# A decoder block in Strassen-like blocks: forming the sums of blocks behind the transpose instead of ahead of it

## The chip, the cores and the metric

The kernel runs on one core of a Trainium2 chip. The metric is the device time of one execution in microseconds, as the median of several runs. The core's engines work side by side, each through its own queue in order, and wait for each other by semaphores: TensorE (PE in the profile; its weight loads are PEld), VectorE (DVE), ScalarE (ACT) and GpSimd (POOL). SyncE (SP) only issues DMAs. SBUF is the on-chip memory, PSUM the eight banks into which TensorE writes; a bank holds 128 x 512 fp32.

## The reference

A block over 1024 tokens of width 1024, all in fp32: half a gated feed-forward layer, a mixer of attention and pooling, and another half feed-forward layer.

```python
h = x
h = h + 0.5 * swiglu(rms_norm(h, ffn1_norm), ffn1_w1, ffn1_w3, ffn1_w2)
u = rms_norm(h, mix_norm)
proj = u @ w_in                      # q, k, v, pooling input, two gates
...
h = h + merged @ w_out
h = h + 0.5 * swiglu(rms_norm(h, ffn2_norm), ffn2_w1, ffn2_w3, ffn2_w2)
return rms_norm(h, final_norm)
```

The three products that matter here are those with a normed `h` on one side: `ffn1_w1`/`ffn1_w3`, `w_in`, and `ffn2_w1`/`ffn2_w3`.

## The kernel before

**Seven products instead of eight.** Each large product is cut into two by two blocks and done with seven block products. The normed activations `X` are cut into `b11`, `b12`, `b21`, `b22`: tokens 0 to 511 or 512 to 1023, columns 0 to 511 (`LOWS`) or 512 to 1023 (`HIGHS`). The first index is the half of the columns, the second the half of the tokens. Needed are `b11`, `b21`, `b22` and four sums: `t1 = b12 - b11`, `t2 = b22 - t1`, `t4 = t2 - b21`, `t3 = b22 - b12`. A product of index `m` uses 1: `b11`, 2: `b21`, 3: `b22`, 4: `t4`, 5: `t1`, 6: `t2`, 7: `t3`, and the products run in the order 1, 6, 2, 7, 5, 4, 3.

**Three matmuls for one.** An operand is rounded to a high part (`hi`, type fp32r, by ScalarE's `AF.Copy`) and a low part (`lo`, the rest, by a subtraction on VectorE or GpSimd). Each product is hi x hi, hi x lo and lo x hi: 12 matmuls of 128 x 128 by 512 for a block of weights (`Sevens.product`, L314). `Sevens.split` (L303 high, L306 low) does this for the weights; inside an entry its low part is always GpSimd's.

**Rows and columns.** The normed rows come with tokens on the partitions, and TensorE needs columns there. So `Rows` transposes 128 x 512 by four TensorE operations against a unit matrix into one PSUM bank (L381), ScalarE writes the high part from the bank (L382), and `lower` writes the low part, bank minus high part, on VectorE (L385).

**An entry.** Each of the three layers begins with an entry. Tokens 0 to 511 (tiles 0 to 3) are normed and transposed first, giving `b11` and `b21`; their rows stay in `h[0]` to `h[3]`. Then `Entry.run` goes over the tiles t = 4 to 7 of the other tokens. While TensorE does products 1 and 2 of the first few weight blocks (`self.todo`: 12 products in the first feed-forward layer, of which 4 are done earlier, 8 in the others), it makes the sums of tile t with those of tile t - 4. The order is written out by hand (`manual_schedule`), and each engine's queue follows it. For one tile it is:

- a product `i`; the statistics of the next tile (`high(t + 1, 0)`, L263 and L264); transposes of `b22` and its high part;
- `t1`, `t2`, `t4` on VectorE (L423 to L425) and `t3` on GpSimd (L426), all on rows in SBUF; `b22`'s low part (L385);
- the weights of product `i + 2` (`operand`, L303, L306), the output of product `i`, the product `k = i + 1`, the weights of product `k + 2`;
- transposes of `t1`, `t2`, `t4`, `t3` with their high parts (L381, L382); scaling of the next tile's rows (`high(t + 1, 1)`, L267, on VectorE); the four low parts (L385); the output of `k`; squares for a later tile.

At t = 6 and 7 the first operands of the products behind the entry are prepared as well (`more`; their sums are L345, L347 and L351).

PSUM has two tags of four banks: `mm` (products 1, 2, 3, 5) and `acc` (the other products, and the transposes). The rows of tiles 0 to 3 are transposed in the last steps of the stage ahead: `rows` in `begin_up1` for the first entry, `rows_first` as tasks of the steps of the first down projection (its matmuls are L706), `rows_first2` and `lower` between the steps of the output projection (L1854).

Of the kernel before, what the change touches and what calls it, by code (L numbers as in the profile page):

```python
# [126 lines left out]
def tile_block(  # L127
# [40 lines left out]
    def bank(tag, name):  # L168
        return psum.tile([P, HALF], F32, tag=tag, name=name)
# [12 lines left out]
    ident = consts.tile([P, P], F32, name="ident")  # L182
# [5 lines left out]
    h = []  # L188
# [80 lines left out]
    def scaled_part(t, c, gain):  # L269
        ve.scalar_tensor_tensor(h[t][:, c], h[t][:, c], inv[t][:, 1:2], gain[:, c], op0=OP.mult, op1=OP.mult)  # L270
# [12 lines left out]
    LOWS, HIGHS = slice(0, HALF), slice(HALF, S)  # L283

    def sums_of_x(pool, name, order, **kw):
        return {
            s: tuple(pool.tile([P, 4, HALF], F32R, name=f"x{part}_{s}_{name}", **kw) for part in ("hi", "lo"))
            for s in order
        }

    class Sevens:


        def __init__(self, name, X, fw, fs=None):
            self.name, self.X, self.fw, self.fs = name, X, fw, fs or fw
            self.n_lo = 0
# [22 lines left out]
    class Quad:  # L319
# [51 lines left out]

    class Rows:


        def __init__(self, X, what, src, t, tag="acc"):
            q = t % 4
            self.hi, self.lo = (v[:, :, q * P:(q + 1) * P] for v in X[what])
            p = bank(tag, f"x_{what}_{t}")
            self.p = p.rearrange("p (k q) -> p k q", k=4)
            for k in range(4):  # L380
                pe.transpose(self.p[:, k, :], src[:, k * P:(k + 1) * P], ident)  # L381
            ac.activation(self.hi, self.p, AF.Copy)  # L382

        def lower(self):
            ve.tensor_tensor(self.lo, self.p, self.hi.bitcast(F32), op=OP.subtract)  # L385

    class Entry:

# [17 lines left out]
        def run(self, high, after, first=0):  # L406


            X = self.sv.X
            y = high(4, 1)  # L410
            for t in range(4, NT):
                i = first + 2 * (t - 4)
                k = i + 1
                self.product(i)
                if t + 1 < NT:
                    high(t + 1, 0)
                lo = self.low[t - 4]
                b11, b21, b12, b22 = lo[:, LOWS], lo[:, HIGHS], y[:, LOWS], y[:, HIGHS]
                s = Rows(X, "b22", b22, t)

                t1, t3 = b11, b21
                t2, t4 = (self.sv.half_tile("s", f"{n}_{t}") for n in ("t2", "t4"))
                ve.tensor_tensor(t1, b12, b11, op=OP.subtract)  # L423
                ve.tensor_tensor(t2, b22, t1, op=OP.subtract)
                ve.tensor_tensor(t4, t2, b21, op=OP.subtract)  # L425
                gp.tensor_tensor(t3, b22, b12, op=OP.subtract)  # L426
                s.lower()
                self.operand(i + 2)
                self.out(i)
                self.product(k)  # L430
                self.operand(k + 2)
                rs = [Rows(X, what, src, t) for what, src in (("t1", t1), ("t2", t2), ("t4", t4), ("t3", t3))]
                if t + 1 < NT:
                    y = high(t + 1, 1)
                for r in rs:
                    r.lower()
                self.out(k)
                after(t)
                if t >= NT - 2:
                    self.more(t - NT + 2)  # L440
# [318 lines left out]
    X = sums_of_x(scope.enter_context(sbuf("x1")), "f1", SUMS)  # L759
# [32 lines left out]
    def begin_up1():  # L792


        load_all()
        idle = bank("mm", "idle")

        def keep_on(n):

            for _ in range(n):  # L800
                pe.matmul(idle[:, :P], ones, ones, start=True, stop=True)

        def widen(b):
            k = slice(4 * b, 4 * b + 4)
            ve.tensor_copy(columns[:, k], gain1[:, k, None].to_broadcast([P, 4, P]))

        def gains(b):

            p = bank("acc", f"gain{b}")
            for k in range(4):  # L810
                pe.transpose(p[:, k * P:(k + 1) * P], columns[:, 4 * b + k], ident)
            return p

        r = {}

        def rows(t, what, c):
            scaled_part(t, c, gain_row)
            r[t] = Rows(X, what, h[t][:, c], t)

        keep_on(12)  # L820
        widen(0)
        squares(0, square)
        widen(1)
        inverse(0)
        g = [gains(b) for b in range(2)]
        keep_on(2)
        ve.tensor_copy(gain_row[:, LOWS], g[0])
        squares(1, square)
        squares(2, square)
        rows(0, "b11", LOWS)  # L830
        inverse(1)
        keep_on(2)
        inverse(2)
        squares(3, square)
        rows(1, "b11", LOWS)
        r[0].lower()
        keep_on(3)
        rows(2, "b11", LOWS)
        inverse(3)
        r[1].lower()  # L840
        keep_on(3)
        pairs = [Pair(sv1, j, sums, True, j == 2) for j in range(3)]
        entry = pre_run(sv1, [(q, m) for m in (1, 2) for q in pairs[:2]] + [(pairs[2], m) for m in (1, 2)],
                        pairs[0], h[:4])
        entry.operand(0)
        rows(3, "b11", LOWS)
        r[2].lower()
        keep_on(2)
        r[3].lower()
        ve.tensor_copy(gain_row[:, HIGHS], g[1])  # L850
        entry.product(0)
        entry.operand(1)

        square2 = columns_tile
        squares(4, square2)
        for t in (0, 1):
            rows(t, "b21", HIGHS)
        entry.product(1)
        entry.out(0)
        entry.operand(2)  # L860
        entry.operand(3)
        inverse(4)
        r[0].lower()
        for t in (2, 3):
            rows(t, "b21", HIGHS)
            r[t - 1].lower()
        entry.product(2)
        entry.out(1)
        squares(5, square2)
        r[3].lower()  # L870
        entry.product(3)
        entry.operand(4)
        entry.out(2)
        entry.operand(5)
        entry.out(3)

        def high(t, part):
            if part == 0:
# [12 lines left out]
        entry.run(high, after, 4)  # L891
        return pairs
# [308 lines left out]
    with sbuf("steps1", "right") as pool:  # L1201
# [30 lines left out]
        def rows_first(t, tag):  # L1232
            rs = [Rows(X_mix, "b11", h[t][:, LOWS], t, tag), Rows(X_mix, "b21", h[t][:, HIGHS], t, tag)]
            for r in rs:
                r.lower()

        def after1(m, t):
            if m == len(DOWN) - 3:
# [53 lines left out]
    with tc.manual_schedule():  # L1292
# [4 lines left out]
        for k in range(len(items) + 4):  # L1297
# [5 lines left out]
            if k < len(items):  # L1303
                q, m = items[k]
# [3 lines left out]
            if k - 1 in results:  # L1308
                q, m = items[k - 1]
# [404 lines left out]
    with tc.manual_schedule():  # L1714
# [44 lines left out]
        q = N // 2  # L1759
# [33 lines left out]
    op = wo.enter_context(sbuf("ops", "right"))  # L1793
# [83 lines left out]
    def scaled2(t):  # L1877
        scaled(t, h[t] if t < 4 else rows_y[t], gain2)

    def lower(rs):  # L1880
        for r in rs:
            r.lower()

    with tc.manual_schedule():
        for k in range(6):
# [59 lines left out]
        raws.load()  # L1945
        r = [rows_first2(t) for t in range(2)]
        step_o(STEPS - 3, range(2))
        lower(r[0])
        lower(r[1])
        r.append(rows_first2(2))  # L1950
        step_o(STEPS - 3, range(2, 4))
        lower(r[2])
        r.append(rows_first2(3))
        adds_o(m - 1, range(2))
        lower(r[3])
        adds_o(m - 1, range(2, 4))
        entry2.operand(0)
        entry2.operand(1)
# [172 lines left out]
```

## Time and profile before

| what | value |
|---|---|
| runs of the kernel | 1960.0, 1959.36, 1956.06 us; median 1959.36 |
| profiled execution, first to last instruction | 1955.6 us, mean granted TensorE clock 0.994 |
| its own time as listed | not marked among the runs; the nearest is 1956.06 |
| TensorE, weight loads | 1914.1, 1579.7 us busy |
| VectorE, ScalarE, GpSimd | 1343.5, 759.4, 741.1 us busy |
| DMA | 333.57 MB, mean 171 GB/s |

The profile comes from one execution. "Busy" counts an instruction from its start to its end, and on VectorE and GpSimd this includes time in which it stands still inside. The time line gives for each group of instructions its start, its length, engine, line, output and inputs, and in brackets how long the engine had been idle and which instruction released it. `x4` means four in a row merged. A table of windows gives, for each stretch of time, its length and the busy time of each engine with the number of instructions, then the granted clock of TensorE and the DMA's share and rate. The first entry's `Entry.run` starts its products at 28.16 us, the mixer's at 666.37 and the second feed-forward layer's at 1297.04.

### The profile page before, as it was taken

What the parts mean: (1) busy time and instruction counts of PE and PEld (TensorE: products, weight loads), DVE (VectorE), ACT (ScalarE), POOL (GpSimd) and SP (SyncE); (2) the same over time, 40 slices, a digit from 0 to 9 for tenths busy, and PEclk for the clock granted to TensorE, in tenths of its full rate; (3) what the DMA queues carried; (4) which work ended last, traced back from release to release, by engine and by line L of the source; (5) the groups of instructions that cost most, each with busy time, mean ns of one, the idle gap of its engine ahead of it and who ended that gap; (6) DMA issues with size and microseconds to landing.
All of it is one profiled execution on the core that took longest, in us unless ns stands there. A gap on an engine that the chain in (4) does not pass through costs nothing. (4 is left out here: it accounts for less than half of the span.)

```text
span 1955.6 us, 25018 instructions
## 1 busy us (share of the span) xinstructions
PE 1914.1 (98%) x8938; PEld 1579.7 (81%) x8938; DVE 1343.5 (69%) x2012; ACT 759.4 (39%) x1361; POOL 741.1 (38%) x557
## 2 busy tenths in 40 slices
PE   9999999999999999999998999999999999999997
PEld 7788888888888887888876878887788888878885
DVE  7776556557686876568774886887665556577766
ACT  6333333334344533334344662253333333333343
POOL 5333333332222444445454365543333333322231
PEclk9999999999999999999998999999999999999999
DMA  4155223336465546765658887643523223454653
GB/s 185 44 194 169 85 86 117 121 124 208 156 246 201 167 120 230 232 220 185 232 218 289 241 241 261 253 161 96 190 102 135 82 87 120 139 204 135 212 195 142
DMA packets 147005, 333.57 MB, mean 171 GB/s; under 512 B 20160, under 2 KB 40896, under 8 KB 145344
## 3 DMA queue, kind: packets, MB, share of 16 engines
q1 hardware_dynamic: 138096, 308.00, 45.9%
q10 hardware_dynamic: 8784, 23.96, 3.5%
q8 instruction: 71, 1.16, 0.2%
q14 instruction: 54, 0.44, 0.1%
HBM read 229.61 MB, written 102.30 MB: 170 GB/s over the span
## 5 line engine op out<-in xcount | busy, mean ns | idle before, releaser
L706 PE MATMUL d_f<-bhi_f,alo_f 128*128 128x512 f32 x616 | 240.8, 391 | 2.4 <-POOL alo_f L668 2.2
L706 PE MATMUL d_f<-bhi_f,ahi_f 128*128 128x512 f32 x616 | 240.9, 391 | 0.2 <-ACT ahi_f L664 0.2
L706 PE MATMUL d_f<-blo_f,ahi_f 128*128 128x512 f32 x616 | 240.0, 390 | 0.0
L668 POOL TENSOR_TENSOR alo_f<-g_f,ahi_f 128x512 fp32r<-128x512 f32 x70 | 99.2, 1434 | 298.5 <-ACT ahi_f L664 289.8
L314 PE MATMUL u_mixm<-xhi_t_mix,wc_mixm 128*128 128x512 f32 x608 | 196.0, 393 | 2.7 <-POOL wc_mixm L306 2.3
L314 PE MATMUL u_mixm<-xhi_b_mix,wc_mixm 128*128 128x512 f32 x456 | 149.3, 393 | 2.0 <-DVE y_m L982 2.0
L706 PEld LDWEIGHTS d_f<-bhi_f,alo_f 128*128 128x128 f32 x616 | 115.7, 188 | 29.0 <-POOL alo_f L668 4.0
L314 PEld LDWEIGHTS u_mixm<-xhi_t_mix,wc_mixm 128*128 128x128 f32 x608 | 113.8, 188 | 29.0 <-POOL wc_mixm L306 4.9
L706 PEld LDWEIGHTS d_f<-bhi_f,ahi_f 128*128 128x128 f32 x616 | 115.8, 188 | 24.1 <-ACT ahi_f L664 0.6
L706 PEld LDWEIGHTS d_f<-blo_f,ahi_f 128*128 128x128 f32 x616 | 115.8, 188 | 23.8
L314 PE MATMUL u_mixm<-xlo_t_mix,wc_mixm 128*128 128x512 f32 x304 | 118.6, 390 | 0.0
L306 POOL TENSOR_TENSOR wc_mixm<-s_mixm,wc_mixm 128x512 fp32r<-128x512 f32 x52 | 75.8, 1459 | 99.7 <-ACT wc_mixm L303 84.0
L314 PEld LDWEIGHTS u_mixm<-xhi_b_mix,wc_mixm 128*128 128x128 f32 x456 | 85.7, 188 | 20.7 <-ACT late_hi L1125 2.8
L303 ACT ACTIVATE wc_mixm<-s_mixm 128x512 fp32r<-128x512 f32 x76 | 47.6, 629 | 122.8 <-DVE s_mixm L347 52.1
L314 PE MATMUL u_mixm<-xlo_b_mix,wc_mixm 128*128 128x512 f32 x228 | 88.9, 390 | 0.0
L664 ACT ACTIVATE ahi_f<-g_f 128x1024 fp32r<-128x1024 f32 x84 | 81.8, 974 | 2.0 <-DMA g_f<-gs_f 2.0
L306 POOL TENSOR_TENSOR wc_mixm<-raw,wc_mixm 128x512 fp32r<-128x512 f32 x40 | 60.4, 1515 | 44.9 <-ACT wc_mixm L303 42.0
L664 ACT ACTIVATE bhi_f<-s_f2w 128x512 fp32r<-128x512 f32 x55 | 32.8, 627 | 97.1 <-DVE s_f2w L684 86.8
L1854 PE MATMUL wo<-w_o,o_hi 128*128 128x512 f32 x224 | 69.3, 391 | 0.0
L314 PEld LDWEIGHTS u_mixm<-xlo_t_mix,wc_mixm 128*128 128x128 f32 x304 | 57.2, 188 | 11.7 <-DVE xlo_t_mix L385 0.2
L664 ACT ACTIVATE bhi_f<-s_f1w 128x512 fp32r<-128x512 f32 x55 | 32.9, 630 | 85.1 <-DVE s_f1w L684 80.2
L1616 PE MATMUL yp<-pool_in,wab 128*128 128x512 f32 x192 | 55.7, 426 | 4.2 <-DMA pool_in<-pool 4.2
(1300 smaller groups left out, 5099.8 us busy)
## 6 DMA issues: line engine op xcount, KB each, us to landing
g_f<-gs_f SPq DMA_DIRECT2D x70, 512.0 KB, 4.5
gs_f<-y_f SPq DMA_DIRECT2D x88, 256.0 KB, 2.3
raw<-in_w2a_dram SPq DMA_DIRECT2D x35, 512.0 KB, 4.1
raw<-in_w2b_dram SPq DMA_DIRECT2D x35, 512.0 KB, 4.0
gs_f<-gb_f SPq DMA_DIRECT2D x46, 256.0 KB, 2.3
raw<-in_w1a_dram SPq DMA_DIRECT2D x22, 512.0 KB, 4.6
raw<-in_w3a_dram SPq DMA_DIRECT2D x22, 512.0 KB, 6.3
raw<-in_w1b_dram SPq DMA_DIRECT2D x22, 512.0 KB, 4.5
```

The costliest lines, as they stand in the source:

```text
L303: ac.activation(w[:, 0], src, AF.Copy)
L306: eng.tensor_tensor(w[:, 1], src, w[:, 0].bitcast(F32), op=OP.subtract)
L314: pe.matmul(p, a, b, start=(start and k == 0 and q == 0), stop=(k == 3 and q == 2), skip_group_check=not start)
L664: ac.activation(hi[:, c], src, AF.Copy)
L668: eng.tensor_tensor(lo[:, d], src[:, o], hi[:, d].bitcast(F32), op=OP.subtract)
L706: pe.matmul(self.banks[m][t], l, r, start=(first and q == 0), stop=(last and q == 2))
L1616: pe.matmul(p, a, b, start=(j == 0), stop=(j == 11))
L1854: pe.matmul(banks[m][t], l, r, start=(st == 0 and j == 0 and q == 0), stop=(st == 1 and j == 1 and q == 2))
```

## The change

In `Entry.run` only `b12` and `b22` of a tile are transposed (both ahead of product `k`), and the sums are formed from the transposed blocks: `t1` from the bank of `b12`, `t2` from the bank of `b22`, `t4` and `t3` in SBUF from `t2`. `t1` and `t2` are then half tiles in SBUF, `t3` and `t4` take the places of `b11` and `b21`. A new class `Parts` takes a high part (ScalarE) and a low part (VectorE, for `t3` GpSimd) from such an fp32 block in SBUF. For that `b11` and `b21` of tiles 0 to 3 must be there transposed: `Rows.keep` copies their bank into `h[t]` on ScalarE, 8 times in each entry. `b22`'s low part moves behind product `k`; one transpose of the first entry takes its bank from `mm`. The formula for `t3` becomes `t2 - b11`, which is the same sum. In the changed program `t1` to `t4` are L441, L442, L445 and L444, `Parts` is L398 (high) and L401 (low), `keep` is L389.

```diff
@@ class Rows
-            p = bank(tag, f"x_{what}_{t}")
+            p = self.flat = bank(tag, f"x_{what}_{t}")
...
+        def keep(self, dst):
+            ac.activation(dst.rearrange("p (k q) -> p k q", k=4), self.p, AF.Copy)
+
+    class Parts:
+        def __init__(self, X, what, src, t, eng):
+            q, self.eng = t % 4, eng
+            self.hi, self.lo = (v[:, :, q * P:(q + 1) * P] for v in X[what])
+            self.src = src.rearrange("p (k q) -> p k q", k=4)
+            ac.activation(self.hi, self.src, AF.Copy)
+
+        def lower(self):
+            self.eng.tensor_tensor(self.lo, self.src, self.hi.bitcast(F32), op=OP.subtract)

@@ Entry.run
-                lo = self.low[t - 4]
-                b11, b21, b12, b22 = lo[:, LOWS], lo[:, HIGHS], y[:, LOWS], y[:, HIGHS]
-                s = Rows(X, "b22", b22, t)
-
-                t1, t3 = b11, b21
-                t2, t4 = (self.sv.half_tile("s", f"{n}_{t}") for n in ("t2", "t4"))
-                ve.tensor_tensor(t1, b12, b11, op=OP.subtract)
-                ve.tensor_tensor(t2, b22, t1, op=OP.subtract)
-                ve.tensor_tensor(t4, t2, b21, op=OP.subtract)
-                gp.tensor_tensor(t3, b22, b12, op=OP.subtract)
-                s.lower()
+                b11, b21 = (self.low[t - 4][:, c] for c in (LOWS, HIGHS))
+                p12 = bank("acc", f"x_b12_{t}")
+                for j in range(4):
+                    c = slice(j * P, (j + 1) * P)
+                    pe.transpose(p12[:, c], y[:, c], ident)
+                s = Rows(X, "b22", y[:, HIGHS], t)
+
+                t1, t2 = (self.sv.half_tile("s", f"{n}_{t}") for n in ("t1", "t2"))
+                ve.tensor_tensor(t1, p12, b11, op=OP.subtract)
+                ve.tensor_tensor(t2, s.flat, t1, op=OP.subtract)
+                rs = [Parts(X, "t2", t2, t, ve)]
+                gp.tensor_tensor(b11, t2, b11, op=OP.subtract)
+                ve.tensor_tensor(b21, t2, b21, op=OP.subtract)
+                rs[0].lower()
                 self.operand(i + 2)
                 self.out(i)
                 self.product(k)
                 self.operand(k + 2)
-                rs = [Rows(X, what, src, t) for what, src in (("t1", t1), ("t2", t2), ("t4", t4), ("t3", t3))]
                 if t + 1 < NT:
                     y = high(t + 1, 1)
+                s.lower()
+                rs = [Parts(X, what, src, t, eng) for what, src, eng in (("t1", t1, ve), ("t4", b21, ve), ("t3", b11, gp))]
                 for r in rs:
                     r.lower()

@@ begin_up1
-        rows(3, "b11", LOWS)
+        rows(3, "b11", LOWS, "mm")
...
         entry.product(0)
         entry.operand(1)
+        for t in range(4):
+            r[t].keep(h[t][:, LOWS])
...
         squares(5, square2)
         r[3].lower()
+        for t in range(4):
+            r[t].keep(h[t][:, HIGHS])
         entry.product(3)
         entry.operand(4)

@@ rows_first, and lower(t, rs) of the output projection alike
             for r in rs:
                 r.lower()
+            for r, c in zip(rs, (LOWS, HIGHS)):
+                r.keep(h[t][:, c])
```

More of the change, by code (lines that the diff above doesn't have):

```diff
@@ L814, in begin_up1, with rows @@
         r = {}
-        def rows(t, what, c):
+        def rows(t, what, c, tag="acc"):
             scaled_part(t, c, gain_row)
-            r[t] = Rows(X, what, h[t][:, c], t)
+            r[t] = Rows(X, what, h[t][:, c], t, tag)
         keep_on(12)
@@ L1878, in scaled2, with lower @@
         scaled(t, h[t] if t < 4 else rows_y[t], gain2)
-    def lower(rs):
+    def lower(t, rs):
         for r in rs:
             r.lower()
+        for r, c in zip(rs, (LOWS, HIGHS)):
+            r.keep(h[t][:, c])
     with tc.manual_schedule():
@@ L1947, in tile_block @@
         step_o(STEPS - 3, range(2))
-        lower(r[0])
-        lower(r[1])
+        lower(0, r[0])
+        lower(1, r[1])
         r.append(rows_first2(2))
         step_o(STEPS - 3, range(2, 4))
-        lower(r[2])
+        lower(2, r[2])
         r.append(rows_first2(3))
         adds_o(m - 1, range(2))
-        lower(r[3])
+        lower(3, r[3])
         adds_o(m - 1, range(2, 4))
```

## The prediction

> **What bounds the kernel now.** I read the page first, then the windows of the three entries, then the order in time inside one of them.
>
> ```profile
> span 1955.6 us, 25018 instructions
> PE 1914.1 (98%) x8938; PEld 1579.7 (81%) x8938; DVE 1343.5 (69%) x2012; ACT 759.4 (39%) x1361; POOL 741.1 (38%) x557
> ...
> core 0: us, PE busy (x) PEld busy (x) DVE busy (x) ACT busy (x) POOL busy (x), PEclk, DMA share, GB/s
> 28.16:59.78 31.62, 31.25 (x178) 26.18 (x176) 27.77 (x37) 18.89 (x36) 20.91 (x15) 1.00 0.15 51
> 666.37:697.59 31.22, 30.87 (x178) 26.33 (x176) 27.20 (x38) 18.91 (x37) 19.58 (x14) 1.00 0.14 51
> 1297.04:1328.86 31.82, 31.18 (x177) 26.25 (x176) 28.18 (x40) 19.08 (x35) 17.41 (x12) 1.00 0.20 70
> ```
>
> Over the whole span TensorE is the bound at 98%. The change touches little besides the three windows, each from an entry's first product to the first product behind it: 94.7 us of the 1955.6. In them VectorE is busy 27 to 28 of 31 to 32 us and GpSimd 17 to 21: two engines close behind the first. Now one token tile of the first entry, in order of time.
>
> ```profile
> 28.16 0.39 PE L314 MATMUL u_f10a<-xhi_b_f,wc_f10a 128*128 128x512 f32 x1
> ...
> 30.88 0.60 PE L381 MATMUL x_b<-ident,x 128*128 128x128 f32 x4
> 31.23 0.48 PE L314 MATMUL u_f10b<-xhi_b_f,wc_f10b 128*128 128x512 f32 x1
> ...
> 38.96 0.48 PE L314 MATMUL u_f11b<-xhi_b_f,wc_f11b 128*128 128x512 f32 x1
> ...
> 40.63 1.30 POOL L426 TENSOR_TENSOR x<-x 128x512 f32<-128x512 f32 x1 [1.13 <-DVE s_f1t L425]
> 41.07 1.94 DVE L267 SCALAR_TENSOR_TENSOR x<-x,nst,gain_ffn 128x1024 f32<-128x1024 f32 x1
> 41.82 0.60 PE L381 MATMUL x_t<-ident,x 128*128 128x128 f32 x4
> 41.89 2.27 POOL L306 TENSOR_TENSOR wc_f12a<-raw,wc_f12a 128x512 fp32r<-128x512 f32 x1
> 43.08 2.48 DVE L385 TENSOR_TENSOR xlo_t_f<-x_t,xhi_t_f 128x512 fp32r<-128x512 f32 x4
> 43.48 0.47 PE L314 MATMUL u_f12a<-xhi_b_f,wc_f12a 128*128 128x512 f32 x1
> 44.12 1.29 POOL L306 TENSOR_TENSOR wc_f12b<-raw,wc_f12b 128x512 fp32r<-128x512 f32 x1
> 44.21 0.30 PEld L314 LDWEIGHTS u_f12a<-xhi_b_f,wc_f12a 128*128 128x128 f32 x2 [0.46 <-POOL wc_f12a L306]
> 46.99 0.48 PE L314 MATMUL u_f12b<-xhi_b_f,wc_f12b 128*128 128x512 f32 x1
> ...
> 54.70 0.48 PE L314 MATMUL u_f12b<-xhi_b_f,wc_f12b 128*128 128x512 f32 x1
> ```
>
> Columns are start, length, engine, line. A product of 12 matmuls takes 2.72 (28.16 to 30.88), four transposes 0.35 (to 31.23), sixteen 1.66 (41.82 to 43.48): a tile needs 2 x 2.72 + 0.35 + 1.66 = 7.45 of TensorE, and the intervals between second products (31.23, 38.96, 46.99, 54.70) are 7.73, 8.03 and 7.71. The 0.46 at 44.21 is TensorE's weight load waiting for the low part of a weight from GpSimd (L306). So GpSimd's queue is already the next bound, by a hair.
>
> Why is one L306 2.27 long and its neighbour 1.29? These rows tell:
>
> ```profile
> 14.65 1.28 POOL L306 TENSOR_TENSOR wc_f10b<-raw,wc_f10b 128x512 fp32r<-128x512 f32 x1 [0.24 <-ACT wc_f10b L303]
> 24.11 1.27 DVE L267 SCALAR_TENSOR_TENSOR x<-x,nst,gain_ffn 128x1024 f32<-128x1024 f32 x1
> 27.22 1.74 POOL L306 TENSOR_TENSOR wc_f10b<-raw,wc_f10b 128x512 fp32r<-128x512 f32 x1
> 27.84 1.67 DVE L425 TENSOR_TENSOR s_f1t<-s_f1t,x 128x512 f32<-128x512 f32 x1
> 39.13 0.69 DVE L424 TENSOR_TENSOR s_f1t<-x,x 128x512 f32<-128x512 f32 x1
> 63.38 1.28 POOL L306 TENSOR_TENSOR wc_f10a<-s_f10a,wc_f10a 128x512 fp32r<-128x512 f32 x1 [4.07 <-ACT wc_f10a L303]
> 63.86 1.35 DVE L306 TENSOR_TENSOR wc_f10a<-s_f10a,wc_f10a 128x512 fp32r<-128x512 f32 x1 [1.28 <-ACT wc_f10a L303]
> ```
>
> Alone, GpSimd's operation takes 1.28, L267 1.27, VectorE's half tile 0.69. Where a VectorE operation with two SBUF inputs meets one of GpSimd, the later is lengthened until the earlier is done: L306 on VectorE (63.86) ends 0.55 after GpSimd's at 64.66, about its own working time, L425 0.55 after 28.96. The four L385 at 43.08, with one input in PSUM, run beside GpSimd (44.12, 1.29) and neither is lengthened. So they take turns whenever both of VectorE's inputs are in SBUF, and not when one is in PSUM. The Trainium skill, "SBUF — State Buffer", section "SBUF: two separate sides", states this as a lock held for the whole instruction by a VectorE operation with two SBUF inputs or by GpSimd; it speaks against this change, whose new low parts have both inputs in SBUF. By that rule each meeting costs what the sum below takes; the trace agrees (1.35 for 0.69).
>
> **The change, part by part.**
>
> *Transposes.* Per tile 20 become 8 (the program's order: four into `x_b12`, four into `x_b22`, none later). Twelve at 1.66/16 are 1.25; over 12 tiles TensorE's work falls by 15.0 us. That is the whole gain, and it counts only where TensorE is the bound.
>
> *The turns.* Spacing of back-to-back operations: VectorE half tile (2.48 - 0.69)/3 = 0.60; GpSimd 1.25, an estimate from its 1.28 less the overlap with the next; L267 1.2. Before, a tile's turn-taking work is t1, t2, t4 (1.8), L267 (1.2), and on GpSimd t3, two L306 (3.75) and a small power (0.5): 7.3, just below TensorE's 7.45. After, t1 and t2 read PSUM and leave the turns, but t4 stays and the low parts of t2, t1, t4 join: 4 x 0.60 + 1.2 = 3.6 on VectorE. GpSimd has t3, two L306 and the low part of t3: 5.0. Together 8.6. VectorE's t1 (0.6), t2 (0.7, behind t1), the product's output and the statistic (0.7) do not need turns, but they stand in VectorE's queue exactly when GpSimd has little ready: t3 waits for t2, and the weights' high parts stand behind the high part of t2 on ScalarE. So a tile takes from 8.6 (full overlap) to 10.6 (none). I take 10.6 for the first entry and 10.0 for the others, whose outputs are mostly ScalarE's: the walk through the queues finds t1 of the next tile waiting for the low part of t4 of this one. TensorE, needing 6.2, waits twice per tile: for the weight's high part, then its low part.
>
> *First interval* (tiles 4 to 5): no backlog. From the second product: t1, t2, t4 1.9, t3 1.25, low part of t2 0.6, L306 1.3 = 5.0; then ten matmuls 2.3 and eight transposes 0.8: 8.1, against 7.73. Ahead of it four transposes more: +0.4.
>
> *End of the entry.* The second product behind the entry needs L351's sum, rounded on ScalarE.
>
> ```profile
> 59.78 0.47 PE L314 MATMUL u_f10a<-xhi_t_f,wc_f10a 128*128 128x512 f32 x1
> ...
> 61.90 0.68 DVE L351 TENSOR_TENSOR s_f10a<-raw,raw 128x512 f32<-128x512 f32 x1
> 62.67 1.15 ACT L303 ACTIVATE wc_f10a<-s_f10a 128x512 fp32r<-128x512 f32 x2 [2.01 <-DVE s_f10a L351]
> 63.35 0.50 PE L314 MATMUL u_f10a<-xhi_t_f,wc_f10a 128*128 128x512 f32 x1 [0.42 <-ACT wc_f10a L303]
> ```
>
> From 54.70 to 63.35 is 8.65 now. After, t1 of tile 7 stands behind tile 6's last low part, L345 and L347 (3.0); then t1, t2 1.3, t4, three low parts, b22's and the output 3.6, three turns given to GpSimd (the next weight, t3, t3's low part) less what b22's covers 3.0, L351 with rounding 1.4: about 12, so +3.4, with a wait of some 4 us on TensorE. The late high parts of t1, t4, t3 cost nothing more: their products come later.
>
> *First entry:* 0.4 + (8.1 - 7.73) + (10.6 - 8.03) + (10.6 - 7.71) + 3.4 = 9.6. The others: 0.6 less on two intervals, 8.4; I take 9.0, between this and the first, their windows being as long. Sum 27.6.
>
> *`keep`, 24 copies on ScalarE.* Each waits for its low part and holds the bank 0.6 longer.
>
> ```profile
> 24.88 0.63 ACT L303 ACTIVATE wc_f10a<-raw 128x512 fp32r<-128x512 f32 x1
> 34.73 2.07 ACT L382 ACTIVATE xhi_t_f<-x_t 128x512 fp32r<-128x512 f32 x4 [1.09 <-PE x_t L381]
> 637.40 1.28 DVE L385 TENSOR_TENSOR xlo_b_mix<-x_b,xhi_b_mix 128x512 fp32r<-128x512 f32 x2
> 638.17 0.47 PE L706 MATMUL d_f<-bhi_f,ahi_f 128*128 128x512 f32 x1
> 1280.67 3.67 DVE L385 TENSOR_TENSOR xlo_b_f<-x_b,xhi_b_f 128x512 fp32r<-128x512 f32 x6
> 1281.41 1.26 PE L381 MATMUL x_b<-ident,h_again 128*128 128x128 f32 x8 [0.81 <-DVE xlo_b_f L385]
> ```
>
> Four copies are 2.07. At 638.17 and 1281.41 TensorE starts as the first L385 releases its bank, so 0.6 more each. In the first entry four stand ahead of the weight at 24.88: its rounding slips by 2, its low part to about 29.0, against 28.6 when it is needed: 0.4. Elsewhere ScalarE has room (39%) and the banks wait for nobody. Sum 1.6. DMAs and SP's queue stay as they are.
>
> *In all* 27.6 + 1.6 = 29.2 on this execution's span of 1955.6. The listed runs are 1956.06 to 1960.0, median 1959.36, 3.8 above the span; I put the sum on the median: 1988.6, say 1989.
>
> **Rivals.**
>
> *Faster, 1948.* TensorE stays the bound if weights are split so far ahead that the turns never reach it. Then 15.0 is saved, less about 4 for waits that stay: 1959.4 - 11 = 1948. It decides itself at a turn time of 6.2 per tile. For it: operands are issued two products ahead, 31 of 31.62 us are TensorE's. Against: 8.6 > 6.2, and the 0.46 wait at a slower pace. 9%. Measured change within 0.2% (4 us, about what a measurement tells from none): both cancel, 3%.
>
> *Milder, 1972.* Only the turns count (8.6 per tile, VectorE's other work hiding beside GpSimd): two intervals +0.7, 0.8 ahead of them, half of the end's 3.4: 3.9 an entry, 11.7 in all, 13 with the openings, 1972. The queue orders speak against it, since t1 and t2 of a tile stand between two turns. 15%, 1964 to 1981.
>
> *The clock, 1997.* Waits could cost the granted clock.
>
> ```profile
> 1056.00:1060.00 4.00, 3.66 (x29) 2.46 (x27) 2.76 (x14) 1.29 (x2) 0.00 (x0) 1.00 1.03 393
> 1060.00:1064.00 4.00, 2.55 (x9) 1.39 (x9) 1.28 (x6) 3.73 (x13) 0.00 (x0) 0.86 1.02 408
> 1064.00:1068.00 4.00, 1.92 (x4) 0.84 (x3) 0.35 (x1) 1.58 (x8) 0.00 (x0) 0.50 1.00 414
> ```
>
> With TensorE busy 2.55 of 4 us (64%) the clock went to 0.86 and then 0.50. After, an entry's tile is 6.2 of 10.6 (58%). Inside the entry TensorE has some 2 us of slack per tile, so half speed hides; behind the last wait nothing hides it: 4 to 6 us at half speed lose 2 to 3 an entry, 6 to 9 in all, 1995 to 1998. The Trainium skill, "TensorE: Matmul & The Clock Gate", "Part 1: The HAM clock gate (the "warmup" mystery)", has the clock halved after an idle window of about 3.4 us; by that rule the 4 us wait would suffice, and the fall above agrees. 20%, 1992 to 2005.
>
> **How the numbers follow.** Forecast 50%, with 1981 to 1996: 5% on the spacings is 1.3 an entry (5% of some 26 us of turns and queue in three tiles), 4 in all, the openings go from 0 to double, and the listed runs themselves spread by 4. Milder 15%, clock 20%, faster 9%, same 3%, worse than 2005 3%. The range 1964 to 2005 leaves out 15%. Faster 0.09, same 0.03, slower 0.88.
>
> **What would show it.** Right: windows of 37 to 38 us where 31 to 32 stood, and 7 instead of 3.6 from their end to the next product; TensorE near 25 us of work in them; 48 transposes fewer per entry; VectorE's new low parts at 1.2 to 1.9 instead of 0.69; TensorE released by L306 and L303 in each tile; a wait of 3 to 5 us at the second product behind each entry. Wrong: low parts near 0.69 beside GpSimd, or windows below 30 us. A granted clock under 1.00 in the windows decides for the clock.

## The result, and the profile after

The changed kernel takes 1990.94 us (median of 4 runs, 1989.67 to 1992.79), the kernel before 1959.42 beside it (median of 4): 1.0168 times as long, 95% interval 1.0154 to 1.0183. The profiled execution is the slowest of the four, 1992.79 us; its span is 35.4 us longer than that of before, while the medians differ by 31.5.

The page of the changed kernel, first lines:

```profile
span 1991.0 us, 24744 instructions
PE 1919.6 (96%) x8794; PEld 1575.1 (79%) x8794; DVE 1365.9 (69%) x2000; ACT 773.5 (39%) x1385; POOL 765.0 (38%) x569
```

TensorE has its 144 transposes fewer (8938 to 8794) and yet no less busy time, since a matmul at a lower clock is counted longer (0.63 us in the time line where it was 0.39). The windows of the three entries, from the first product to the first behind the entry (columns: window, length, then busy time and count of PE, PEld, DVE, ACT, POOL, then the granted clock):

```profile
28.25:66.03 37.78, 29.93 (x130) 22.58 (x128) 32.64 (x34) 18.24 (x35) 27.71 (x19) 0.91 0.14 43
677.27:713.59 36.32, 28.75 (x129) 21.74 (x127) 31.98 (x33) 17.88 (x35) 25.20 (x17) 0.95 0.11 44
1320.79:1358.36 37.57, 30.45 (x130) 22.94 (x128) 33.27 (x35) 18.14 (x33) 23.72 (x15) 0.91 0.22 73
```

They were 31.62, 31.22 and 31.82 long. TensorE, which filled them, now waits for 7 to 8 us of each (length less busy time); GpSimd is busy 24 to 28 us where it was 17 to 21, and the clock is no longer 1.00. One tile of the first entry in order of time (the same tile of which the prediction shows the old form; columns are start, length, engine, line, and in brackets the wait and what ended it):

```profile
43.95 0.69 DVE L445 TENSOR_TENSOR x<-s_f1t,x 128x512 f32<-128x512 f32 x1
43.99 1.78 POOL L444 TENSOR_TENSOR x<-s_f1t,x 128x512 f32<-128x512 f32 x1 [0.84 <-DVE s_f1t L442]
44.61 1.72 DVE L401 TENSOR_TENSOR xlo_t_f<-s_f1t,xhi_t_f 128x512 fp32r<-128x512 f32 x1
...
45.15 0.50 PE L314 MATMUL u_f12a<-xhi_b_f,wc_f12a 128*128 128x512 f32 x1 [1.51 <-ACT wc_f12a L303]
...
45.74 1.72 POOL L306 TENSOR_TENSOR wc_f12a<-raw,wc_f12a 128x512 fp32r<-128x512 f32 x1
...
46.25 2.29 DVE L267 SCALAR_TENSOR_TENSOR x<-x,nst,gain_ffn 128x1024 f32<-128x1024 f32 x1
...
47.42 2.28 POOL L306 TENSOR_TENSOR wc_f12b<-raw,wc_f12b 128x512 fp32r<-128x512 f32 x1
...
47.51 0.73 PE L314 MATMUL u_f12a<-xhi_b_f,wc_f12a 128*128 128x512 f32 x2 [1.63 <-POOL wc_f12a L306]
48.47 0.68 DVE L385 TENSOR_TENSOR xlo_b_f<-x_b,xhi_b_f 128x512 fp32r<-128x512 f32 x1
49.07 1.18 DVE L401 TENSOR_TENSOR xlo_t_f<-s_f1t,xhi_t_f 128x512 fp32r<-128x512 f32 x1
49.66 1.73 POOL L401 TENSOR_TENSOR xlo_t_f<-x,xhi_t_f 128x512 fp32r<-128x512 f32 x1
50.17 1.76 DVE L401 TENSOR_TENSOR xlo_t_f<-x,xhi_t_f 128x512 fp32r<-128x512 f32 x1
51.86 0.68 DVE L522 TENSOR_TENSOR y_f<-u_f11b,y_f 128x512 f32<-128x512 f32 x1
...
54.03 0.69 DVE L445 TENSOR_TENSOR x<-s_f1t,x 128x512 f32<-128x512 f32 x1
```

Read the ends of the DVE and POOL rows (start plus length): 44.64, 45.77, 46.33, 47.46, 48.54, 49.70, 50.25, 51.39, 51.93. The two engines strictly alternate. Each end follows the other engine's end by 0.54 to 0.56 for VectorE's half tiles and by 1.08 to 1.16 for L267 and GpSimd's operations, which is about the own work of each, so an operation starts its work when the other engine's ends. From 43.95 to 51.93 there is no gap: 8.0 us of turns. Only L385, whose input is a PSUM bank, runs beside GpSimd at 0.68. Behind the turns VectorE still has the output, the statistic, t1 and t2, 2.1 us, before t4 of the next tile starts at 54.03: 10.1 us a tile. TensorE's two waits of the tile, 1.51 and 1.63, lie inside.

Where the 35.4 us of the profiled span lie is found by comparing the start of the same matmul in both traces (the transposes left out, 8602 matmuls stand in both, in the same order but for four):

| stretch | longer by |
|---|---|
| the three entries, first product to second product behind | 8.9 + 8.0 + 8.6 = 25.5 |
| behind the first entry, to 77 us | 1.3 |
| openings of f1, mix, f2 | 0.1 + 0.6 + 0.6 = 1.3 |
| between the mix entry and f2's opening | 4.3 |
| behind f2's entry, to the end | 3.0 |

### The profile page after: what moved, and what is told of

Its sections match the earlier page's. It is cut to its first block, busy times and chain, and to the rows that moved or that the text cites. A ratio compares the mean times of both kernels' runs of the same rounds, so it can differ in the third digit from the quotient of the medians.

```text
span 1991.0 us, 24744 instructions
## 1 busy us (share of the span) xinstructions
PE 1919.6 (96%) x8794; PEld 1575.1 (79%) x8794; DVE 1365.9 (69%) x2000; ACT 773.5 (39%) x1385; POOL 765.0 (38%) x569
## 5 line engine op out<-in xcount | busy, mean ns | idle before, releaser
L306 POOL TENSOR_TENSOR wc_mixm<-s_mixm,wc_mixm 128x512 fp32r<-128x512 f32 x52 | 74.7, 1438 | 100.7 <-ACT wc_mixm L303 88.2
L303 ACT ACTIVATE wc_mixm<-s_mixm 128x512 fp32r<-128x512 f32 x76 | 47.6, 629 | 133.2 <-DVE s_mixm L347 56.4
L306 POOL TENSOR_TENSOR wc_mixm<-raw,wc_mixm 128x512 fp32r<-128x512 f32 x40 | 61.2, 1534 | 44.7 <-ACT wc_mixm L303 42.0
```

Of the source, the lines that this page charges most:

```text
L303: ac.activation(w[:, 0], src, AF.Copy)
L306: eng.tensor_tensor(w[:, 1], src, w[:, 0].bitcast(F32), op=OP.subtract)
```

## The experiments

Each kernel's time is given as its ratio to the kernel before, run beside it on the same chip (medians of before 1955.83, 1957.88 and 1957.86 in the three groups). "Entry" is from an entry's first product to the second product behind it, in the profiled execution.

| kernel | median us | ratio, 95% | entries f1, mix, f2 | sum |
|---|---|---|---|---|
| before | | 1 | 35.19, 34.22, 35.40 | 104.8 |
| changed | 1990.94 | 1.0168 (1.0154 to 1.0183) | 44.08, 42.20, 44.03 | 130.3 |
| sums_in_psum | 1972.13 | 1.0079 (1.0067 to 1.0091) | 41.00, 39.20, 39.46 | 119.7 |
| after_filled | 1983.46 | 1.0134 (1.0118 to 1.0150) | 44.12, 42.28, 44.24 | 130.6 |
| more_transposes | 1982.39 | 1.0131 (1.0118 to 1.0144) | 44.08, 42.25, 44.17 | 130.5 |
| before_fewer_transposes | 1976.44 | 1.0104 (1.0085 to 1.0122) | 40.18, 40.52, 43.03 | 123.7 |
| weights_first | 1982.24 | 1.0124 (1.0110 to 1.0139) | 42.59, 41.33, 42.18 | 126.1 |
| psum_weights_first | 1966.67 | 1.0046 (1.0033 to 1.0059) | 37.41, 36.23, 38.19 | 111.8 |
| psum_filled | 1968.00 | 1.0052 (1.0038 to 1.0067) | 40.18, 39.68, 42.22 | 122.1 |
| before_weights_first | 1966.23 | 1.0044 (1.0032 to 1.0056) | 37.63, 37.24, 38.67 | 113.5 |
| no_keeps | 1986.65 | 1.0154 (1.0141 to 1.0167) | 44.45, 44.44, 44.58 | 133.5 |
| third_entry_only | 1965.06 | 1.0041 (1.0025 to 1.0057) | 35.18, 34.35, 44.59 | 114.1 |

The theory under test is the prediction's: an entry is set by the turns of VectorE and GpSimd and by what stands in VectorE's queue around them. Its rivals are that VectorE's amount of work alone does it, and that the granted clock does it.

**sums_in_psum: the operands of the sums and low parts out of the turns.** t3 also goes from GpSimd to VectorE, and ScalarE copies `b22` to SBUF.

```diff
-t1, t2 = (half_tile("s", ...) for n in ("t1", "t2"))
+b22 = half_tile("s", ...)
+t1, t2, t4 = p12, bank("acc", ...), bank("acc", ...)
+ac.activation(b22, s.flat, AF.Copy)        # ahead of b22's high part
 ve.tensor_tensor(t1, p12, b11, op=OP.subtract)
-ve.tensor_tensor(t2, s.flat, t1, op=OP.subtract)
+ve.tensor_tensor(t2, b22, t1, op=OP.subtract)
 ...
-gp.tensor_tensor(b11, t2, b11, op=OP.subtract)
+ve.tensor_tensor(b11, t2, b11, op=OP.subtract)
-ve.tensor_tensor(b21, t2, b21, op=OP.subtract)
+ve.tensor_tensor(t4, t2, b21, op=OP.subtract)
 ...
```

> The changed kernel, with the operands of the sums in other places and nothing else moved: t1 is written over b12's transposed bank, t2 and t4 into PSUM banks of their own, b22 is copied to SBUF by ScalarE first (an instruction has one PSUM input at most), and t3 is formed by VectorE from t2's bank instead of by GpSimd. Every VectorE operation of the sums and low parts so has an input in PSUM. VectorE has one operation more per tile, ScalarE one copy more. Turns (VectorE operations with two SBUF inputs and GpSimd exclude each other): VectorE's low parts come back to 0.69 us beside GpSimd, each entry's window falls from 36 to 38 us to 30 to 32, and the time is 1952 to 1962. Queue (VectorE simply has more work per tile, wherever its inputs lie): the windows stay at 36 to 38 or grow by half a microsecond per tile, 1991 to 1998. Clock (most of the loss is the granted clock after waits): the windows shorten only as far as the waits go; with the waits it stays above 1980.

It took 17 us less than the changed kernel (0.0089 of 1957), and 10 more than the upper end of what the turns were expected to leave; the windows to the first product behind fell to 34 to 36 us, not to 30 to 32. The groups of the low parts' line, in the changed kernel (durations are least, median, most, in ns):

```profile
L401 DVE TENSOR_TENSOR xlo_t_f<-s_f1t,xhi_t_f x8: 1168/1694/1734, 34.5 to 68.1; 128x512 fp32r<-128x512 f32 x8
L401 DVE TENSOR_TENSOR xlo_t_f<-x,xhi_t_f x4: 679/1766/1769, 40.1 to 69.7; 128x512 fp32r<-128x512 f32 x4
```

and the same line, now L405, with the sums in PSUM:

```profile
L405 DVE TENSOR_TENSOR xlo_t_f<-x_t,xhi_t_f x16: 674/680/684, 35.5 to 1342.4; 128x512 fp32r<-128x512 f32 x16
L405 DVE TENSOR_TENSOR xlo_t_f<-x_b,xhi_t_f x8: 674/677/684, 39.0 to 1341.8; 128x512 fp32r<-128x512 f32 x8
```

A low part falls from 1.7 us to 0.68 and no longer varies, although VectorE has one operation more per tile. So it was the place of the operands, not the amount of work, that made these operations long; the rival of the queue's length alone is out. How much of the 17 us comes from t3 alone, which leaves GpSimd one operation less per tile, the run does not tell. And the entries stay 14.9 us over before in sum, at clocks of 0.88 to 0.92, and TensorE waits in them for a weight's high part (0.99 us) and low part (0.62), as in the changed kernel.

**after_filled and more_transposes: the changed kernel, with work for TensorE in its waits.**

```diff
+def fill(self, p):                          # twelve transposes of the identity
+    for j in range(12):
+        pe.transpose(p[:, j % 4 * P:(j % 4 + 1) * P], ident, ident)
 # tile's end, behind operand(k + 2), both kernels (more_transposes: of y)
+self.fill(extra)
 # after_filled alone: in product(i), behind the second matmul, from the second tile on
+self.fill(extra)
```

> The changed kernel with work for TensorE in its two waits of each tile: twelve transposes of the identity into a bank that nobody reads at the tile's end (ahead of the wait for a weight's high part) and, from the second tile of an entry on, twelve more behind the second matmul of the first product (ahead of the wait for its low part). 1.25 us each, where the waits were 1.5 to 1.65. The clock in the entries should stay at 1.00 but for their ends. Turns and queue (an entry is set by VectorE and GpSimd; the clock's loss hides in the waits): the entries, from their first product to the second product behind them, stay within 2 us of 44, and only the stretches outside gain: 1980 to 1986. Clock (half speed behind the waits makes up much of the loss): each entry falls by 3 to 5 us, to 39 to 41, and the time to 1968 to 1978. TensorE-bound after all: 20 us more, 2010.

> The changed kernel with twelve transposes more per tile, into a bank that nobody reads, where the kernel before had its sixteen (behind the second product): TensorE gets the 15 us of work back that the change took away. Turns and queue: TensorE is not the bound in the entries, the work goes into its waits, and the time is within 2 us of 1991. Rival, TensorE still bounds the entries: 15 more, 2006. Clock: less idle time keeps the granted clock up behind the waits, 3 to 8 us less, 1983 to 1988.

The windows of the entries of after_filled, to the second product behind:

```profile
28.76:72.88 44.12, 40.74 (x226) 33.50 (x224) 38.27 (x39) 20.79 (x40) 30.03 (x20) 0.96 0.11 37
676.57:718.85 42.28, 38.49 (x225) 32.37 (x223) 37.16 (x37) 21.05 (x41) 27.70 (x18) 1.00 0.11 38
1313.41:1357.65 44.24, 40.67 (x225) 34.00 (x224) 39.04 (x40) 20.95 (x38) 26.35 (x17) 0.94 0.18 62
```

TensorE does 84 transposes more per entry, the clock is 1.00 in the mix entry (0.92 in the changed kernel) and elsewhere below it only at the end, and each entry is as long as in the changed kernel within about 0.2 us. The entries of more_transposes, with 48 transposes more and other clocks (0.92, 1.00, 0.93), are as long too. So within the entries of the changed kernel neither TensorE's work nor its clock sets the time: both hide in the waits, as the turns would have it. The times of both kernels fell by 7 us all the same, all of it behind or between the entries. For after_filled the turns expected that. For more_transposes they did not: its time is what the rival of the clock had named for the stretches behind the waits. I come back to that.

**before_fewer_transposes: the gain alone.**

```diff
-rs = [Rows(X, what, src, t) for what, src in (("t1", t1), ("t2", t2), ("t4", t4), ("t3", t3))]
+rs = [Rows(X, "t1", t1, t)]
+rs += [Rows(X, what, None, t, like=rs[0]) for what in ("t2", "t4", "t3")]
```

> The kernel before with the gain of the change alone: t2, t4 and t3 take their high and low parts from t1's transposed bank, so twelve transposes per tile are left out (and the values of these three are wrong); every operation on the other engines stays. Turns (before, they take 7.3 us a tile, just under TensorE's 7.45): the saving is not to be had, since GpSimd's low parts come next; 0 to 1 us an entry, 1956 to 1959. Rival, TensorE alone bounds the entries: 5 us an entry, 1944.

Both theories missed: it did not gain and did not stay, it lost 20.6 us (1.0104). The time line in its first entry, and two windows around its longest wait:

```profile
43.36 2.24 POOL L306 TENSOR_TENSOR wc_f12a<-raw,wc_f12a 128x512 fp32r<-128x512 f32 x1
...
45.66 0.72 PE L314 MATMUL u_f12a<-xhi_b_f,wc_f12a 128*128 128x512 f32 x2 [3.82 <-POOL wc_f12a L306]
```

```profile
43.40:46.80 3.40, 1.15 (x5) 0.99 (x6) 3.40 (x6) 1.10 (x3) 3.40 (x2) 1.00 0.00 0
46.80:50.20 3.40, 3.40 (x12) 2.71 (x11) 2.71 (x6) 0.01 (x1) 1.52 (x3) 0.50 0.02 5
```

TensorE waits there 3.82 us in one piece. In the 3.40 us from 43.40 it is busy 1.15, and the next 3.40 us it works at half clock. TensorE came to this wait 2.35 us earlier than in the kernel before (the product's first matmul is at 41.13 instead of 43.48), but GpSimd came to this low part 1.47 later (43.36 instead of 41.89). The reason for the second stands further up, here in the kernel before and then in this run:

```profile
35.36 2.48 DVE L385 TENSOR_TENSOR xlo_t_f<-x_t,xhi_t_f 128x512 fp32r<-128x512 f32 x4 [0.26 <-ACT xhi_t_f L382]
```

```profile
34.76 2.07 ACT L382 ACTIVATE xhi_t_f<-x_t 128x512 fp32r<-128x512 f32 x4 [1.09 <-PE x_t L381]
36.85 2.48 DVE L385 TENSOR_TENSOR xlo_t_f<-x_t,xhi_t_f 128x512 fp32r<-128x512 f32 x4 [1.73 <-ACT xhi_t_f L382]
```

With all four parts in one bank, VectorE's first low part starts behind the fourth high part (36.83) and no longer behind the first, in all twelve tiles. Here VectorE is 1.5 us later by it, and so is what stands behind in its queue and in GpSimd's. So the edit did more than leave transposes out.

The entries' clocks are 0.92, 0.89 and 0.85 and the entries 18.9 us longer in sum. A clock of 0.92 can cost at most 8% of its entry, and so on: 14 us in the three, an estimate from these clocks and lengths. The clock alone is thus not the loss, and the run does not part its share from that of the later low parts. What twelve transposes fewer do by themselves, it does not show.

**weights_first: the changed kernel with a weight ahead of t2's parts.**

```diff
+self.operand(i + 2)
 rs = [Parts(X, "t2", t2, t, ve)]
 ...
 rs[0].lower()
-self.operand(i + 2)
```

> The changed kernel with the next tile's first weight ahead of t2's parts and t3 in the queues of ScalarE and GpSimd (the line self.operand(i + 2) moved up by four lines), nothing else. The prediction's step that the weights' high parts stand behind t2's high part: TensorE's waits for L303 in the tile go, a tile gains 0.5 to 1 us, but GpSimd's t3 and the last low parts come later; the entry 1.5 to 2 us shorter each, the time 5 us below the changed kernel's, 1983 to 1986. Rival, the turns alone set the pace and order changes nothing: within 2 us of the changed kernel, 1987 to 1991.

1.0124: 8.6 us less than the changed kernel, of which 4.2 in the entries (1.5, 0.9 and 1.9, where 1.5 to 2 each were expected). The rival that order changes nothing is out; the other 4.4 lie outside the entries, where the edit touches nothing. Two of TensorE's waits inside the first entry:

```profile
44.26 0.74 PE L314 MATMUL u_f12a<-xhi_b_f,wc_f12a 128*128 128x512 f32 x2 [0.46 <-POOL wc_f12a L306]
48.83 0.63 PE L437 MATMUL x_b<-ident,x 128*128 128x128 f32 x4 [1.96 <-DVE x L267]
```

The 1.51 for ScalarE's high part is gone, the 1.63 for the low part is 0.46, and 1.96 for L267, the scaling of the next rows, has come in their place: VectorE's own operation in the turns. So the order of the queues is worth a part of the loss.

**psum_weights_first and psum_filled: both cures, and then filled.** The first is sums_in_psum with the move of weights_first; the second adds `self.fill(extra)` at the tile's end.

> The kernel with the sums in PSUM (as in the run before of that name) and the next tile's first weight ahead of t2's parts. There TensorE waited up to 1.0 us for that weight's high part and 0.6 for its low part. Queue order: these waits go, with them the halved clock inside the entries, and each entry comes within 1 us of the kernel before or below it: 1956 to 1962. Clock (TensorE's work is now too small for the pace that VectorE sets, so idle time stays somewhere and the clock falls): as with the sums in PSUM alone, 1966 to 1972.

> As psum_weights_first, with twelve transposes of the identity more at each tile's end, into a bank that nobody reads: TensorE has as many transposes as in the kernel before, and none of its results is used more. If what is left of the loss is the granted clock: the clock stays at 1.00 in the entries and the time falls to 1954 to 1960. If VectorE's and GpSimd's queues set the pace: no gain over psum_weights_first, within 2 us. If TensorE's work is the bound there: 3 to 10 us slower than psum_weights_first.

psum_weights_first is the best form of the change that I found, 1.0046, and still slower than before. Its time lies in the range named for the clock (1966 to 1972) and not in that named for the queue order, and the clock in its entries is 0.97, 0.95 and 0.91. Its intervals between second products in the first entry are 6.90, 7.95 and 7.96, against 7.73, 8.03 and 7.71: the turns' cost is gone, and no gain has come in its place, with VectorE busy 28.5 of 37.4 us. It loses at the ends: 0.9 us ahead of the first second product, where four transposes more stand, and the most behind the last tile:

```profile
61.55 0.47 PE L314 MATMUL u_f10a<-xhi_t_f,wc_f10a 128*128 128x512 f32 x1 [3.63 <-ACT xhi_t_f L402]
```

The first product behind the entry waits 3.63 us; in the kernel before, the wait there, of the transposes just ahead, is 0.35. The high part that ended last before 61.55 is t4's, which this product does not need, and t2's low part ended at 61.40; which of them holds it, the profile does not settle. Both come behind t1 of the last tile, which VectorE reaches at 56.89 after three low parts, L345 and L347.

Filling (psum_filled) brought the clock to 1.00 in two entries and to 0.96 in the third, and made the entries 10.3 us longer: the added transposes wait 1.2 to 1.5 us in each tile of the first entry for a bank that a low part has to release, and everything behind them waits too. The time is 1.3 us more, within the two intervals, so the entries' loss came back outside them. By the number this is the queues' "no gain, within 2 us", but no theory had the two parts that cancel here, and the run says nothing on the clock in this form. A filling at another place was not tried, so how much of the 9 us that psum_weights_first is over before comes from the clock stays open.

**before_weights_first: the same move in the kernel before.**

```diff
+self.operand(i + 2)
 gp.tensor_tensor(t3, b22, b12, op=OP.subtract)
 s.lower()
-self.operand(i + 2)
```

> The kernel before with the next tile's first weight ahead of t3 in GpSimd's queue and ahead of b22's low part (the line self.operand(i + 2) moved up by two lines). There TensorE waited 0.46 us for that weight's low part. Queue order: the wait goes and an entry gains up to 1 us, 1955 to 1958. Rival, t3 is what comes next on the path (it is transposed last, and its sum on GpSimd now starts 1.3 us later): the sixteen transposes wait and each entry loses 1 to 3 us, 1961 to 1967.

The rival, at the upper end of what it named: 8.4 us slower, each entry 2.4 to 3.3 longer at a clock of 1.00, and the wait has the name foretold:

```profile
36.68 0.66 PE L381 MATMUL x_t<-ident,x 128*128 128x128 f32 x4 [0.72 <-POOL x L427]
```

L427 is t3 there. In the kernel before, GpSimd's queue has little to spare: the operation that was moved back is now the one that is waited for.

**no_keeps and third_entry_only: the small terms.** no_keeps leaves the 24 `keep` calls away; third_entry_only has the old `Entry.run` for f1 and mix and no copies there.

> The changed kernel without the 24 copies of keep: left out is the move of b11 and b21, transposed, into h, so the sums are formed from the rows that stand there. All else is the same. The prediction's term: the copies delay three openings by 0.4, 0.6 and 0.6 us, so 1.6 less, 1989.3. Rival, copies free: 1991. Rival, each of the 24 copies (about 0.6 us on ScalarE) stands on the path: 14 less, 1977.

> The change in the third entry alone: f2 as in the changed kernel, with its eight copies of keep; the first entry and the mix entry as in the kernel before, without copies. The sum by entries: 8.6 us for f2 and 0.6 for its opening, and the two other entries and all stretches between as before: 9 to 10 us over the kernel before, 1966 to 1969. Rival, the loss outside the entries (7 us in the profile of the changed kernel) comes from the clock wherever the program stands, not from the entries ahead: part of it is here too, 12 to 16 us over.

Without the copies the time is 2.7 us lower by the ratios, whose intervals overlap; the profiles show it more finely. The openings of mix and f2 lose 0.63 and 0.64 in the changed kernel and 0.01 and 0.00 without the copies, at this row of the changed kernel and its like. (Its mix entry is 2.2 longer than the changed kernel's, at a clock of 0.85, so a halved clock in the wrong place of an entry can show.)

```profile
648.99 0.50 PE L726 MATMUL d_f<-bhi_f,ahi_f 128*128 128x512 f32 x1 [0.46 <-ACT h L389]
```

With the change in f2 alone the profile shows 9.2 for the entry and 0.6 for its opening; the time was 7.2 us over before (4.9 to 11.2 by the interval), a little under the 9 to 10 expected. In the profiled execution the stretch from 740 to 1260 us is 3 us shorter than before; one profile does not tell whether that is chance. The 12 to 16 us of the rival did not come. So f2's entry costs alone about what it costs behind the two others (8.6).

## Why the prediction was right, point by point

**The time and the signs.** 1989 was forecast for the median, 1990.94 came. Windows of 37 to 38 us were named, and 7 from their end to the next product; 36.3 to 37.8 and 5.9 to 6.5 came. VectorE's new low parts were to take 1.2 to 1.9; most take 1.2 to 1.8. TensorE was to wait for L306 and L303 in each tile; in the first entry it waits for L306 in each, and for L303 by more than 0.3 us in one (at the last it is an output on ScalarE, L493, that holds it 2.01).

**The transposes save nothing.** They went (x178 to x130 in each window), and TensorE was not the bound any more: more_transposes put them back without lengthening an entry. Whether they could be had on their own stays open, since before_fewer_transposes changed more than that.

**The turns.** Forecast: 8.6 us of turns a tile, 10.6 with VectorE's other work, that work hardly overlapping. Measured: 8.0 and 10.1, and the 2.1 between as the walk had it, t1 of the next tile behind the low part of t4 of this one. The mechanism held; the turns came 0.6 under because each spacing was put a little high (0.60, 1.25 and 1.2, where 0.55, 1.14 and 1.08 came). The small power on GpSimd, 0.5 in the sum of before, was missing without a word in the sum of after. That did no harm: in the trace it runs beside t1 (52.67, 0.55 long), inside the 2.1. The Trainium skill, "SBUF — State Buffer", section "SBUF: two separate sides", speaks of a lock for the whole instruction that goes to whichever of the two starts first; the chain of ends from 44.64 to 51.93 and the 0.68 of sums_in_psum agree.

**The intervals.** 8.1, 10.6, 10.6 and 12 at the end were forecast for the first entry; 8.42, 10.09, 12.50 and 9.11 came. The last two are shifted against each other by a halved clock (below), and their sum, 21.6, is 1 under the 22.6 forecast. In after_filled, the first of the two at full clock, they are 10.06 and 11.57. The entries' sum is 25.5 against 27.6.

**The end of the entry.** A wait of 3 to 5 us at the second product behind was forecast. There are 3.1 us of it, but in two pieces, since the first product behind already waits for t2's low part:

```profile
67.66 0.50 PE L314 MATMUL u_f10a<-xlo_t_f,wc_f10a 128*128 128x512 f32 x1 [1.24 <-DVE xlo_t_f L401]
...
72.33 0.50 PE L314 MATMUL u_f10a<-xhi_t_f,wc_f10a 128*128 128x512 f32 x1 [1.88 <-ACT wc_f10a L303]
```

The prediction had called the late high parts free, thinking of t1, t4 and t3; t2, whose product comes first, it had left out there.

**The copies.** 1.6 forecast, 1.3 in the profile.

**The clock.** This rival had 20%, and its sign in the profile was wrongly chosen. The text said that a granted clock under 1.00 in the windows would decide for it. The clock fell to 0.91 to 0.95 there, and after_filled shows that it cost these entries nothing. The price at the entries' ends, 2 to 3 us each, was 1.3 behind the first and none behind the others. But the forecast case had no clock in it at all, and in the profiled execution 7.3 us lie between and behind the entries (4.3 + 3.0), where the change touches nothing, part of it at half clock. In the medians it is about half of that: 31.5 - 25.5 - 1.3 - 1.3 = 3.4. One such place, the changed kernel first, then the same matmuls before:

```profile
1779.80:1783.20 3.40, 1.75 (x6) 0.85 (x6) 3.40 (x3) 1.85 (x4) 3.20 (x2) 1.00 0.70 250
1783.20:1786.60 3.40, 3.40 (x8) 2.75 (x9) 2.78 (x4) 0.87 (x2) 0.00 (x0) 0.50 0.67 222
```

```profile
1745.53:1748.95 3.42, 2.69 (x12) 1.82 (x12) 3.42 (x3) 1.98 (x3) 3.18 (x2) 1.00 0.66 231
1748.95:1752.36 3.41, 3.41 (x16) 2.79 (x17) 2.65 (x4) 0.88 (x3) 0.00 (x0) 1.00 0.56 224
```

The place is passed at full clock before and at half after, but the clock is not where it begins. Just ahead of it VectorE waits for a DMA, again in the changed kernel first:

```profile
1776.30 0.69 DVE L565 TENSOR_TENSOR gb_f<-y_f,y_f 128x512 f32<-128x512 f32 x1 [2.93 <-DMA gs_f<-gb_f]
```

```profile
1741.89 0.69 DVE L545 TENSOR_TENSOR gb_f<-y_f,y_f 128x512 f32<-128x512 f32 x1 [0.87 <-DMA gs_f<-gb_f]
```

The wait is 2.06 longer, so TensorE's next operands come later and it is busy 1.75 instead of 2.69; then the clock halves. The place is 3.7 us longer, of which 3.4 us at half clock can be 1.7 at most. Over the twelve profiles this wait for the DMA lies between 0.87 and 2.93; why, no run settles. Outside the entries and the 6 us behind them, and ahead of the last 15 us, the half clock comes to 13.7 us in the profile of before, 27.3 in that of the changed kernel, and 3.4 to 6.8 in the three filled kernels. Between the mix entry and f2's opening the filled ones are even 4 to 7 us shorter than the kernel before. Why, with work that differs only in the entries, is open; one profile of each doesn't tell chance from cause. So the forecast was near partly by luck, because misses cancelled: the entries came out 2.1 under and the copies 0.3, while this came 3.4 over and the stretch behind the first entry 1.3.

So of the 25.5 us that the entries lost, the operands' place, with t3's move to VectorE, is the largest part (10.7, from 130.3 to 119.7), the order of a weight the next (7.8, to 111.8; alone, in weights_first, it was 4.2), and 7.0 stay in the best form.

## What to carry to other kernels

Moving work off the busiest engine gains only what the next one has to spare: here, by the prediction's count, the turns of VectorE and GpSimd (7.3 us a tile) had 0.15 less than TensorE (7.45), and an edit that saved TensorE 1.25 gave them two operations more. When an edit turns PSUM operands into SBUF operands, count the operations that now take turns, and try whether the sum can stay in PSUM (1.7 us back to 0.68 here). A low granted clock in a window proves nothing by itself: fill the waits, and see whether the window shortens.

## What the runs showed of the hardware that I had not expected

That the clock halves without a window in which TensorE is idle. After 3.40 us in which TensorE was busy 1.15 or 1.75 us the next 3.40 us ran at half clock; after 2.69 they did not (the rows above). About half busy it goes both ways. In the changed kernel's first entry 1.78 was enough to keep the clock:

```profile
45.80:49.21 3.41, 1.78 (x8) 1.43 (x8) 3.41 (x4) 2.90 (x6) 3.41 (x2) 1.00 0.00 0
49.21:52.62 3.41, 3.41 (x20) 2.89 (x19) 3.41 (x5) 0.60 (x1) 2.18 (x2) 1.00 0.02 5
```

The half-clock stretches last 3.41 us or whole multiples of it (6.83, 13.65) and lie on one grid within an execution, so that the same wait may fall into one piece of the grid or be shared by two. The Trainium skill, "TensorE: Matmul & The Clock Gate", "Part 1: The HAM clock gate (the "warmup" mystery)", has free-running windows of this length, which agrees, and halves the clock after an idle one; by these rows a window need not be idle. The prediction read its own rows as agreeing with the idle window; in the 3.41 us ahead of that drop, at 1062.87, TensorE was busy 1.76, so they did not.

And that the turns are strict: in the tile shown, eight of the nine operations that alternate are longer than their own time (1.72 for 0.69, 2.28 for 1.28), yet the two engines' work simply adds up, 8.0 us without a gap. Each engine by itself looks well used; only the ends read together show that one of the two is waiting wherever their operations overlap.
